# A two-layer transformer trunk on one core: the first sublayer's shift and scale as columns with the features in the partitions, applied to x r transposed beforehand

## The chip, the core and the metric

The kernel runs on one core of a Trainium2 chip. Its five engines have queues of their own and wait for each other through semaphores: TensorE (PE in the profile, its weight loads PEld), VectorE (DVE), ScalarE (ACT), GpSimd (POOL) and SyncE (SP), which here issues all DMAs. The metric is the time of one execution in microseconds (us). Everything is float32. A product of two large matrices is made of three passes with operands split into a rounded high part and the rest, the low part (type fp32r, "hi" and "lo" below); a matmul of plain float32 operands takes two passes on PE.

## What is computed

A trunk of two layers, 256 tokens of 1024 features, each layer of three sublayers: a SwiGLU, a mixer, a SwiGLU. Each sublayer normalises x, modulates it with a shift and a scale that come from one conditioning vector c, and adds its gated output to x. What the change touches is the modulation of the very first sublayer:

```
mod = silu(c) @ ada_w[i] + ada_b[i]                      # (1, 9 * 1024)
sh0, sc0, g0, sh1, sc1, g1, sh2, sc2, g2 = jnp.split(mod, 9, axis=-1)
h = rmsnorm(x, pre_norm[i, 0]) * (1.0 + sc0) + sh0       # rmsnorm(x, g) = x * rsqrt(mean(x*x) + eps) * g
y = swiglu(h, ffn_w_gate[i, 0], ffn_w_up[i, 0], ffn_w_down[i, 0])
x = x + 0.5 * g0 * rmsnorm(y, post_norm[i, 0])
```

## The kernel before

The 256 tokens are two tiles of 128 (t = 0, 1), X[0] and X[1], with the tokens in the partitions. A product needs its input transposed: HT holds h with the features in the partitions, for each tile, hi and lo, and eight blocks k of 128 features. `mm` (L267) multiplies HT's block k with a weight tile `whl`: three passes for each half of 480 columns. A weight block of 256 rows arrives by one DMA as `raw`; ACT casts each 128 rows to hi (L234) and DVE subtracts for lo (L235), into `whl`. There are 5 `raw` and 7 `whl` buffers.

The first sublayer is special. Its shift and scale are needed before any product can start, and they are sums over 1024 rows of 2048 columns of `ada_w` (8.4 MB). They are worked out in four pieces of 256 features (`first_part`, `PIECES`), so that products of the blocks k = 2q, 2q+1 can start after piece q. A piece is loaded as four tiles `fraw` by eight DMAs of 256 KB with rows of 1 KB. Eight rows j of each partition are weighted with silu(c) (`scond`): DVE accumulates 5 or 6 of them in `facc` (L375, L379), PE the other 2 or 3 (`PEJ`) directly, with `scond` as the stationary operand spread over 128 columns (L377), so that the sum over the partitions comes out the same in all 128 partitions. Another float32 matmul adds the bias (L369), one with `ones` sums `facc` (L380). Shift and scale then lie along the free axis, 256 columns, equal in all partitions: DVE forms g = (1 + scale) pre_norm (L381, pre_norm broadcast into 128 partitions as `pnb`), ACT copies the shift (L382). For each tile t, `modulated` makes h = x g r + shift on DVE (L414, L415; r is the root from `normed`: squares on ACT, L404, L406, and a power on POOL, L407), PE transposes it block by block (L418), and `split` writes hi (ACT, L393) and lo (DVE, L394) into HT.

The products of the sublayer's first part, in the order of the code: for each k, `gate` (960 columns) and `upA` (480 columns), for the two tiles one after the other; then `upB` (the other 480 columns of up) for all k. Each is 18 passes of 480 columns for a k of gate and upA together, 144 in all, and 48 for upB.

Tiles come from pools; the order of the instructions on each engine is set by a list scheduler when the kernel is built, from the order of the code, priorities and its own estimates. Each engine then runs its list strictly in order. Background work for the later sublayers (`ada_items`: on POOL the memsets of `pg`, `g`, `sh`, L302; DMAs of `araw`; DVE, L311) is spread over the kernel by `background`.

## Time and profile before

| what | before |
|---|---|
| three runs, us | 1059.56, 1059.62, 1062.03 (median 1059.62) |
| the profiled execution, us | 1058.01 |
| its span from first to last instruction, us | 1056.2 |
| PE busy | 1015.5 us, 96% of the span |
| DVE, ACT, POOL busy | 75%, 50%, 4% |
| DMA | 249 MB, 68% of 16 engines' span |
| first product of the sublayer on PE | 19.77 us |
| last product of gate and upA | 69.6 us |

The page lists engines by busy time, then groups of instructions by line, and the chain of work that ended last. The timeline gives single instructions; a stretch of time gives each engine's busy time in it. A matmul's time in the profile overlaps that of the next one, so the pace of a row of passes is read from the distance of their starts, not from the mean of one.

### The profile page before, as it was taken

What the parts mean: (1) busy time and instruction counts of PE and PEld (TensorE: products, weight loads), DVE (VectorE), ACT (ScalarE), POOL (GpSimd) and SP (SyncE); (2) the same over time, 40 slices, a digit from 0 to 9 for tenths busy, and PEclk for the clock granted to TensorE, in tenths of its full rate; (3) what the DMA queues carried; (4) which work ended last, traced back from release to release, by engine and by line L of the source; (5) the groups of instructions that cost most, each with busy time, mean ns of one, the idle gap of its engine ahead of it and who ended that gap; (6) DMA issues with size and microseconds to landing.
All of it is one profiled execution on the core that took longest, in us unless ns stands there. A gap on an engine that the chain in (4) does not pass through costs nothing.

```text
span 1056.2 us, 15311 instructions
## 1 busy us (share of the span) xinstructions
PE 1015.5 (96%) x5936; PEld 873.6 (83%) x5936; DVE 788.6 (75%) x1121; ACT 523.8 (50%) x834; POOL 45.0 (4%) x49
## 2 busy tenths in 40 slices
PE   5999999989999999999999999999999899999997
PEld 2689997769778789998878999887777678999875
DVE  5769887989976977877688967767988575765643
ACT  3354534455575654543455544346477555544432
POOL 1000000001000200000030000001000120000000
PEclk9999999999999999999999999999999999999999
DMA  9959899986443477988757979956653443778431
GB/s 315 343 147 322 313 321 378 347 293 218 148 142 128 155 273 247 352 286 291 271 193 260 314 257 316 316 208 236 260 200 118 153 134 115 243 235 261 183 117 40
DMA packets 93732, 249.48 MB, mean 236 GB/s; under 512 B 6084, under 2 KB 24652, under 8 KB 93660
## 3 DMA queue, kind: packets, MB, share of 16 engines
q1 hardware_dynamic: 93660, 248.52, 68.1%
q8 instruction: 46, 0.75, 0.3%
q14 instruction: 26, 0.21, 0.1%
HBM read 247.44 MB, written 1.05 MB: 235 GB/s over the span
## 4 chain that ended last, share of the span: by engine, by line
PE 57%; issue 20%; DVE 4%; ACT 3%; POOL 2%; DMA 1%; POOLq 0%; DVEq 0%; ACTq 0%
PE ydown L267 15%; PE up L282 9%; PE gate L282 8%; PE gate L267 3%; PE up L267 3%; PE projQd L267 2%; PE projQ L267 2%; PE projV L267 2%; PE projA L267 2%; PE projK L267 2%; PE ydsa L267 1%; POOL rstd L407 1%; DVE whl L235 1%; PE dsaO L752 1%; PE ydiff L267 1%
## 5 line engine op out<-in xcount | busy, mean ns | idle before, releaser
L235 DVE TENSOR_TENSOR whl<-raw,whl 128x1024 fp32r<-128x1024 f32 (+3 forms) x216 | 245.7, 1150 | 98.5 <-ACT whl L234 97.7
L234 ACT CAST whl<-raw 128x1024 fp32r<-128x1024 f32 (+3 forms) x216 | 211.8, 995 | 190.1 <-PE ydown L267 89.5
L282 PE MATMUL gate<-HT,wj 128*128 128x256 f32 x1344 | 166.2, 284 | 1.5 <-DVE wj L212 1.4
L212 DVE TENSOR_TENSOR wj<-raw,wj 128x1024 fp32r<-128x1024 f32 x112 | 134.7, 1221 | 43.1 <-ACT wj L211 42.8
L211 ACT CAST wj<-raw 128x1024 fp32r<-128x1024 f32 x112 | 116.4, 1050 | 100.3 <-DMA raw<-in_ffn_w_up_dram 21.5
L282 PEld LDWEIGHTS gate<-HT,wj 128*128 128x128 f32 x1344 | 163.4, 192 | 2.2 <-DVE wj L212 1.9
L282 PE MATMUL up<-HT,wj 128*128 128x256 f32 x1344 | 164.4, 283 | 0.0
L282 PEld LDWEIGHTS up<-HT,wj 128*128 128x128 f32 x1344 | 162.8, 192 | 0.4
L267 PE MATMUL ydown<-whl,ffj 128*128 128x512 f32 x672 | 157.0, 390 | 2.2 <-DVE whl L235 2.2
L267 PEld LDWEIGHTS ydown<-whl,ffj 128*128 128x128 f32 x672 | 125.7, 188 | 30.6 <-DVE whl L235 3.1
L267 PE MATMUL gate<-whl,HT 128*128 128x480 f32 x384 | 94.3, 392 | 0.4 <-ACT HT L393 0.2
L267 PE MATMUL ydown<-whl,ffa 128*128 128x512 f32 (+1 forms) x368 | 89.3, 393 | 1.9 <-ACT whl L234 1.9
L267 PEld LDWEIGHTS gate<-whl,HT 128*128 128x128 f32 x384 | 72.2, 191 | 16.6 <-ACT HT L393 2.7
L267 PEld LDWEIGHTS ydown<-whl,ffa 128*128 128x128 f32 (+1 forms) x368 | 67.9, 188 | 19.7 <-issue 3.6
L311 DVE SCALAR_TENSOR_TENSOR pg<-araw,scond,pg 128x1024 f32<-128x1024 f32 x48 | 61.4, 1280 | 6.4 <-DMA araw<-in_ada_w_dram 5.8
L267 PE MATMUL up<-whl,HT 128*128 128x480 f32 x288 | 66.0, 381 | 0.0
L267 PEld LDWEIGHTS up<-whl,HT 128*128 128x128 f32 x288 | 53.5, 188 | 8.4 <-ACT sg L512 0.5
L311 DVE SCALAR_TENSOR_TENSOR g<-araw,scond,g 128x1024 f32<-128x1024 f32 x40 | 51.2, 1281 | 7.8 <-DMA araw<-in_ada_w_dram 7.4
L311 DVE SCALAR_TENSOR_TENSOR sh<-araw,scond,sh 128x1024 f32<-128x1024 f32 x40 | 51.2, 1280 | 1.3 <-DMA araw<-in_ada_w_dram 0.8
L468 POOL TENSOR_TENSOR rstdy<-rstdy,mhalf 128x1 f32<-128x1 f32 x12 | 10.2, 850 | 824.2 <-ACT rstdy L467 824.2
L267 PE MATMUL projV<-whl,HT 128*128 128x512 f32 x96 | 28.4, 416 | 0.0
L267 PE MATMUL projQ<-whl,HT 128*128 128x512 f32 x96 | 27.6, 415 | 0.0
(224 smaller groups left out, 1090.7 us busy)
## 6 DMA issues: line engine op xcount, KB each, us to landing
araw<-in_ada_w_dram SPq DMA_DIRECT2D x64, 1024.0 KB
raw<-in_ffn_w_down_dram SPq DMA_DIRECT2D x40, 1024.0 KB
raw<-in_ffn_w_gate_dram SPq DMA_DIRECT2D x56, 512.0 KB
raw<-in_ffn_w_up_dram SPq DMA_DIRECT2D x56, 512.0 KB
raw<-in_ffn_w_gate_dram SPq DMA_DIRECT2D x16, 960.0 KB
raw<-in_diff_w_in_dram SPq DMA_DIRECT2D x12, 1024.0 KB
raw<-in_ffn_w_up_dram SPq DMA_DIRECT2D x12, 960.0 KB
fraw<-in_ada_w_dram SPq DMA_DIRECT2D x32, 256.0 KB
```

The costliest lines, as they stand in the source:

```text
L211: nc.scalar.copy(hl[0], raw)
L212: nc.vector.tensor_tensor(hl[1], raw, hl[0].bitcast(F32), op=OP.subtract)
L234: nc.scalar.copy(hl[:, 0, 0:n], raw[:, j, 0:n])
L235: nc.vector.tensor_tensor(hl[0:r, 1, 0:n], raw[0:r, j, 0:n], hl[0:r, 0, 0:n].bitcast(F32), op=OP.subtract)
L267: nc.tensor.matmul(acc[:, hf, 0:n], lhs, rhs, start=(first and hf not in seen), stop=(last and i % 3 == 2))
L282: nc.tensor.matmul(a[:, b, :], w[:, wp, j, b * 128:(b + 1) * 128], HT[:, :, hp, k0 + j, :], start=(first and j == 0 and i == 0 and b % 2 = ...
L311: nc.vector.scalar_tensor_tensor(a, raw[:, j, :], scond[:, 2 * i + j:2 * i + j + 1], a, op0=OP.mult, op1=OP.add)
L407: nc.gpsimd.tensor_tensor(r, r, mhalf[:, 0:1], op=OP.pow)
L468: nc.gpsimd.tensor_tensor(r, r, mhalf[:, 0:1], op=OP.pow)
L752: nc.tensor.matmul(flat(O)[:, h * 64:(h + 1) * 64], ptb[u][:, i * nb + b, :], v[:, b, :], start=(b == 0), stop=(b == nb - 1), skip_group_c ...
```

## The change

Shift and scale are no longer worked out as rows that are equal in all partitions, but as columns: one number for each feature, with the feature in the partition. `column_sums` makes `fraw` or `facc` the stationary operand, block by block of 128 features, and the single column `scond[:, j]` or `ones` the moving one, so each gives one column of shift or scale (a 128x1 matmul). `PEROWS` says which rows j go to PE: one of eight in the first two pieces, two of eight in the others. There are five pieces now: 128, 128, 256, 256, 256 features; the DMAs of the first two carry 128 KB with rows of 512 bytes.

The bias and pre_norm come as 24 rows of 128 (`frows`) and are turned into columns by one transpose (`fcol`). x is loaded first, multiplied by r (`xr`) and transposed by PE, 16 blocks, before the first piece (`first_x`); ACT copies the blocks to `xT`. A block of h is then one DVE operation on `xT` with scale and shift as per-partition scalars, for both tiles together (128x256); ACT writes hi and DVE lo from it. The transposes between the pieces (L418), the row operations L381, L382, L414, L415, the broadcast load of pre_norm and the tiles `g`, `sh`, `pn` of this sublayer are gone.

```
-PEJ = [3, 2, 2, 3]
-PIECES = [(i * 256, 256) for i in range(4)]
+PIECES = [(0, 128), (128, 128), (256, 256), (512, 256), (768, 256)]
+PEROWS = [(7,), (7,), (3, 7), (3, 7), (3, 7)]
...
         a = tmp("facc", (128, 2, n))
-        ps = flat(tr_tile("ps_mod0"))[:, 0:2 * n]
-        r = f0 // 256
-        nc.tensor.matmul(ps, ident[0:4, r:r + 1].to_broadcast([4, 128]),
-                         m["rows"][:, :, f0 % 256:f0 % 256 + n], start=True, stop=False)
+        ps = flat(tr_tile("ps_mod0"))[:, 0:2 * m]
+        begun = False
+
+        def column_sums(block, by, stop=False):
+
+            nonlocal begun
+            for part in range(2):
+                for k in range(m):
+                    o = part * m + k
+                    nc.tensor.matmul(ps[:, o:o + 1], block[:, part, k * 128:(k + 1) * 128], by, start=not begun,
+                                     stop=stop, skip_group_check=True)
+                    begun = True
+
+        first = True
         for j in range(8):
             rj = raws[j // 2][:, j % 2]
             sj = scond[:, j:j + 1]
-            if j == 0:
+            if j in PEROWS[q]:
+                column_sums(rj, sj)
+            elif first:
                 nc.vector.tensor_scalar(a, rj, sj, None, op0=OP.mult)
-            elif j >= 8 - PEJ[q]:
-                nc.tensor.matmul(ps, sj.to_broadcast([128, 128]), flat(rj), start=False, stop=False)
+                first = False
             else:
                 nc.vector.scalar_tensor_tensor(a, rj, sj, a, op0=OP.mult, op1=OP.add)
-        nc.tensor.matmul(ps, ones, flat(a), start=False, stop=True)
-        nc.vector.scalar_tensor_tensor(m["g"][:, c], ps[:, n:2 * n], 1.0, pn, op0=OP.add, op1=OP.mult)
-        nc.scalar.copy(m["sh"][:, c], ps[:, 0:n])
+        column_sums(a, ones[:, 0:1], stop=True)
+        k0 = f0 // 128
+        mc = small.tile([128, 2, m], F32, name="modc")
+        nc.vector.tensor_tensor(mc, ps.rearrange("p (a k) -> p a k", a=2), fcol[:, 0:2, k0:k0 + m], op=OP.add)
+        nc.vector.tensor_tensor(mc[:, 1], mc[:, 1], fcol[:, 2, k0:k0 + m], op=OP.mult)
+        h = tmp("h", (128, m, 2, 128))
+        for k in range(m):
+            nc.vector.tensor_scalar(h[:, k], FIRST["xT"][(k0 + k) // 4][:, (k0 + k) % 4], mc[:, 1, k:k + 1],
+                                    mc[:, 0, k:k + 1], op0=OP.mult, op1=OP.add)
+            hi, lo = HT[:, :, 0, k0 + k, :], HT[:, :, 1, k0 + k, :]
+            nc.scalar.copy(hi, h[:, k])
+            nc.vector.tensor_tensor(lo, h[:, k], hi.bitcast(F32), op=OP.subtract)
...
+    def first_x():
...
+        for u in range(2):
+            r, _ = normed(u)
+            xr = tmp("xr")
+            nc.vector.tensor_scalar(xr, X[u][:, 0:D], r, None, op0=OP.mult)
+            for q in range(2):
+                ps = tr_tile("ps_x")
+                for j in range(4):
+                    nc.tensor.transpose(ps[:, j, :], xr[:, (4 * q + j) * 128:(4 * q + j + 1) * 128], ident)
+                nc.scalar.copy(xT[q][:, :, u, :], ps)
```

Where the scheduler puts the work, at three places (line numbers of after are those of the changed file).

DVE at the start of the kernel, before: from the constants to the first weight tile (`facc` is the first piece's sum).

```order
L375 TENSOR_SCALAR facc<-fraw,scond 128x512
L379 SCALAR_TENSOR_TENSOR facc<-fraw,scond,facc 128x512 x3
L100 TENSOR_SCALAR ident<-jp 128x128
L103 TENSOR_SCALAR negc<-jp 128x128
L379 SCALAR_TENSOR_TENSOR facc<-fraw,scond,facc 128x512
L381 SCALAR_TENSOR_TENSOR g<-ps_mod_125,pnb_110 128x256
L414 TENSOR_TENSOR h<-x_79,g 128x256
L414 TENSOR_TENSOR h<-x_81,g 128x256
L415 SCALAR_TENSOR_TENSOR h<-h,rstd,sh 128x256 x2
L235 TENSOR_TENSOR whl<-raw,whl 128x960
```

DVE at the same place after: `xr` is x r, `whl` are the first four weight tiles of gate and up and then two of the next gate block, `modc` the first piece's columns.

```order
L450 TENSOR_SCALAR xr<-x_79,rstd 128x1024
L445 COPY fcol<-ps_f 128x24
L446 TENSOR_SCALAR fcol<-fcol 128x8
L450 TENSOR_SCALAR xr<-x_81,rstd 128x1024
L235 TENSOR_TENSOR whl<-raw,whl 128x960 x2
L235 TENSOR_TENSOR whl<-raw,whl 128x480 x2
L378 TENSOR_SCALAR facc<-fraw,scond 128x256
L235 TENSOR_TENSOR whl<-raw,whl 128x960
L381 SCALAR_TENSOR_TENSOR facc<-fraw,scond,facc 128x256
L235 TENSOR_TENSOR whl<-raw,whl 128x960
L381 SCALAR_TENSOR_TENSOR facc<-fraw,scond,facc 128x256 x5
L385 TENSOR_TENSOR modc<-ps_mod_175,fcol 128x2
```

The first piece's sum stood ahead of all weight tiles and now stands behind four of them, with two more in its midst.

POOL at the start, before (`rstd` is r of a tile; `pg`, `g`, `sh` the background's memsets).

```order
L98 IOTA jp 128x128
L407 TENSOR_TENSOR rstd<-rstd,mhalf 128x1 x2
L302 MEMSET pg 128x1024
L302 MEMSET g 128x1024
L302 MEMSET sh 128x1024
```

POOL after.

```order
L98 IOTA jp 128x128
L418 TENSOR_TENSOR rstd<-rstd,mhalf 128x1
L302 MEMSET pg 128x1024
L302 MEMSET g 128x1024
L302 MEMSET sh 128x1024
L418 TENSOR_TENSOR rstd<-rstd,mhalf 128x1
```

The second tile's r now stands behind three memsets.

ACT from the first blocks of HT on, before (`sh` is the shift of pieces 2 to 4; casts of 960 columns are gate's weight tiles, of 480 columns up's).

```order
L234 CAST whl<-raw 128x960
L382 COPY sh<-ps_mod_219 128x256
L234 CAST whl<-raw 128x960
L234 CAST whl<-raw 128x480 x2
L393 CAST HT<-ps_x 128x256 x2
L234 CAST whl<-raw 128x960
L382 COPY sh<-ps_mod_313 128x256
L234 CAST whl<-raw 128x960
L234 CAST whl<-raw 128x480 x2
L393 CAST HT<-ps_x 128x256 x2
L234 CAST whl<-raw 128x960 x2
L382 COPY sh<-ps_mod_407 128x256
```

ACT after, from the casts of the second gate block on (HT rows: pieces 1 and 2, then 3 and 4, then 5).

```order
L234 CAST whl<-raw 128x960 x2
L392 CAST HT<-h 128x2x128 x2
L234 CAST whl<-raw 128x480 x2
L392 CAST HT<-h 128x2x128 x4
L234 CAST whl<-raw 128x960 x2
L234 CAST whl<-raw 128x480 x2
L392 CAST HT<-h 128x2x128 x2
L234 CAST whl<-raw 128x960 x2
L234 CAST whl<-raw 128x480 x5
```

The casts of the third and the fourth gate block (960 columns) stood ahead of the HT blocks of the piece before their use and now stand behind them.

## Rows read from the trace of the kernel before

**Rows 1.** The first part of the page: busy time of each engine over the whole span, its share, and its instructions.
```profile
PE 1015.5 (96%) x5936; PEld 873.6 (83%) x5936; DVE 788.6 (75%) x1121; ACT 523.8 (50%) x834; POOL 45.0 (4%) x49
```

**Rows 2.** Busy time of each engine in stretches of 20 us (PE, PEld, DVE, ACT, POOL; then the granted clock of TensorE, the busy share of the DMA engines and GB/s).
```profile
100.00:120.00 20.00, 20.00 (x166) 19.83 (x165) 18.13 (x24) 8.01 (x10) 0.00 (x0) 1.00 0.81 283
...
140.00:160.00 20.00, 18.57 (x150) 18.12 (x149) 18.45 (x19) 8.68 (x10) 0.00 (x0) 1.00 0.99 356
160.00:180.00 20.00, 17.89 (x92) 14.27 (x91) 14.49 (x14) 9.33 (x11) 0.00 (x0) 1.00 1.03 369
180.00:200.00 20.00, 19.12 (x82) 14.81 (x81) 18.03 (x17) 8.28 (x9) 0.00 (x0) 1.00 0.99 382
```

**Rows 3.** The same view in a stretch of 4 us, where the DMA engines fill up again.
```profile
136.00:140.00 4.00, 4.00 (x36) 4.00 (x35) 2.79 (x3) 2.32 (x3) 0.00 (x0) 1.00 1.01 363
```

**Rows 4.** The same view in stretches of 2 us: the rates of single kinds of transfer (x with rows of 4 KB at 12 us, the slices of `ada_w` with rows of 1 KB at 28 us, a weight block with rows of 3.75 KB at 34 us) and the time after the last of the first transfers.
```profile
12.00:14.00 2.00, 2.00 (x3) 0.97 (x4) 0.00 (x0) 0.14 (x1) 0.00 (x0) 1.00 1.03 418
...
28.00:30.00 2.00, 2.00 (x7) 1.02 (x6) 0.14 (x1) 0.20 (x1) 0.00 (x0) 1.00 1.11 350
...
34.00:36.00 2.00, 2.00 (x11) 1.75 (x10) 2.00 (x6) 0.00 (x0) 0.00 (x0) 1.00 1.03 398
...
54.00:56.00 2.00, 2.00 (x9) 1.43 (x8) 1.20 (x2) 0.75 (x2) 0.00 (x0) 1.00 0.00 0
```

**Rows 5.** The timeline of the first 20 us (start, time, engine, line, operation, out<-in, count; in brackets the idle time before and what ended it).
```profile
1.60 3.99 SPq L361 DMA_DIRECT2D fraw<-in_ada_w_dram  x8
...
5.36 0.49 DVE L375 TENSOR_SCALAR facc<-fraw,scond 128x512 f32<-128x512 f32 x1 [3.81 <-DMA fraw<-in_ada_w_dram]
...
11.87 4.38 PE L377 MATMUL ps_mod<-fraw,scond 128*128 128x512 f32 x6
...
13.86 0.63 ACT L404 ACTIVATE junk<-x 128x512 f32<-128x512 f32 x1 [11.29 <-DMA x<-in_x_dram]
...
15.23 0.30 ACT L406 ACTIVATE rstd<-ss 128x1 f32<-128x1 f32 x1
...
15.61 0.56 POOL L407 TENSOR_TENSOR rstd<-rstd,mhalf 128x1 f32<-128x1 f32 x1 [14.54 <-ACT rstd L406]
...
17.66 0.95 POOL L302 MEMSET pg<- 128x1024 f32 x1
...
18.55 0.95 POOL L302 MEMSET g<- 128x1024 f32 x1
...
19.77 2.02 PE L267 MATMUL gate<-whl,HT 128*128 128x480 f32 x8
```

**Rows 6.** The timeline from 50 to 70 us: the last piece of the modulation, its transposes and what follows on PE.
```profile
51.06 2.84 PE L377 MATMUL ps_mod<-fraw,scond 128*128 128x512 f32 x6
...
63.55 1.27 PEld L267 LDWEIGHTS gate<-whl,HT 128*128 128x128 f32 x6
...
64.85 0.62 PEld L267 LDWEIGHTS upB<-whl,HT 128*128 128x128 f32 x3
...
68.97 0.82 PE L267 MATMUL upA<-whl,HT 128*128 128x480 f32 x3
```

**Rows 7.** One stretch, 19.77 to 69.60 us, five times, each row of the instructions that touch one tile alone: `gate`, `upA`, `upB`, `ps_mod`, `ps_x` in this order (length; PE busy with the count of matmul passes; PEld; the others).
```profile
19.77:69.60 49.83, 26.79 (x96) 17.64 (x96) 2.07 (x4) 1.00 0.81 273
...
19.77:69.60 49.83, 13.63 (x48) 9.01 (x48) 0.66 (x1) 1.00 0.81 273
...
19.77:69.60 49.83, 3.34 (x12) 2.36 (x13) 0.00 (x0) 1.00 0.81 273
...
19.77:69.60 49.83, 12.66 (x26) 4.49 (x26) 1.27 (x3) 1.12 (x3) 1.00 0.81 273
...
19.77:69.60 49.83, 2.19 (x12) 1.33 (x12) 3.00 (x8) 2.52 (x7) 1.00 0.81 273
```

**Rows 8.** A short stretch with the instructions of tile `dsaO` alone (length; PE, PEld, DVE busy with counts), and below it the group of this tile's weight loads by form (count, busy us, mean ns).
```profile
296.52:296.91 0.39, 0.39 (x4) 0.39 (x4) 0.00 (x0) 1.00 0.00 0
...
L752 PEld LDWEIGHTS dsaO<-vdsa,PP 128*128 128x128 f32 x96 | 12.4, 191 | 1.8 <-ACT PP L746 0.8
```

**Rows 9.** Groups by form on DVE (line, operation, shapes, count, busy us, mean ns, idle time before). L853 is an operation with two per-partition scalars on one column.
```profile
L235 DVE TENSOR_TENSOR whl<-raw,whl 128x960 fp32r<-128x960 f32 x56 | 64.2, 1154 | 18.3 <-ACT whl L234 18.2
...
L235 DVE TENSOR_TENSOR whl<-raw,whl 128x480 fp32r<-128x480 f32 x16 | 9.9, 653 | 2.7 <-ACT whl L234 2.6
...
L853 DVE TENSOR_SCALAR rsd<-rsd,sums,lamneg 128x1 f32<-128x1 f32 x16 | 4.3, 272 | 0.3
...
L415 DVE SCALAR_TENSOR_TENSOR h<-h,rstd,sh 128x256 f32<-128x256 f32 x8 | 3.5, 478 | 0.0
...
L394 DVE TENSOR_TENSOR HT<-ps_x,HT 128x256 fp32r<-128x256 f32 x8 | 3.0, 417 | 0.0
```

**Rows 10.** Groups by form on ACT (the same columns).
```profile
L234 ACT CAST whl<-raw 128x960 fp32r<-128x960 f32 x56 | 55.3, 996 | 35.5 <-PE gate L267 19.3 <-DMA raw<-in_ffn_w_gate_dram 10.7 <-PE up L267 3.3
...
L234 ACT CAST whl<-raw 128x480 fp32r<-128x480 f32 x16 | 9.1, 595 | 3.2 <-PE gate L267 1.4 <-DVE whl L235 0.8 <-ACT whl L234 0.7
...
L393 ACT CAST HT<-ps_x 128x256 fp32r<-128x256 f32 x8 | 2.9, 374 | 2.5 <-PE ps_x L418 2.4
```

**Rows 11.** The timeline around 236 us, where PE comes back after an idle time, and under it the busy time of the engines from 236 to 240 us (columns as in the stretches above; PEclk is the last number but two).
```profile
236.22 1.77 PE L418 MATMUL ps_x<-ident,h 128*128 128x128 f32 x8 [3.39 <-DVE h L415]
...
236.00:240.00 4.00, 3.78 (x16) 3.54 (x17) 3.73 (x7) 2.64 (x5) 1.47 (x2) 0.61 0.55 218
```

More of the change, by code (lines that the diff above doesn't have):

```diff
@@ L347, in first_part @@
         f0, n = PIECES[q]
+        m = n // 128
         c = slice(f0, f0 + n)
-        m = MOD[0]
-        if q == 0:
-            m["rows"] = big("abrow", (4, 2, 256))
-            nc.sync.dma_start(m["rows"], ada_b[0:1, 0:2048].rearrange("o (a q n) -> (o q) a n", a=2, n=256))
-            mod_tile(0, "g")
-            mod_tile(0, "sh")
-            m["pn"] = big("pnb0", (128, 1024))
         raws = []
@@ L362, in first_part @@
             raws.append(raw)
-        if f0 % 512 == 0:
-            nc.sync.dma_start(m["pn"][:, f0:f0 + 512], bcast_rows(pre_norm[0, 0, f0:f0 + 512], 512))
-        pn = m["pn"][:, c]
         a = tmp("facc", (128, 2, n))
-        ps = flat(tr_tile("ps_mod0"))[:, 0:2 * n]
-        r = f0 // 256
-        nc.tensor.matmul(ps, ident[0:4, r:r + 1].to_broadcast([4, 128]),
-                         m["rows"][:, :, f0 % 256:f0 % 256 + n], start=True, stop=False)
+        ps = flat(tr_tile("ps_mod0"))[:, 0:2 * m]
[9 more added lines that the diff above has]
+        first = True
         for j in range(8):
@@ L421, in trunk @@
     FIRST = {}
+    fcol = consts.tile([128, 3, 8], F32, name="fcol")
+    def first_x():
+        for u in range(2):
+            nc.sync.dma_start(X[u][:, 0:D], x[0, u * 128:(u + 1) * 128, :])
+        rows = big("frows", (24, 128))
+        nc.sync.dma_start(rows[0:16, :], ada_b[0:1, 0:2048].rearrange("o (r n) -> (o r) n", n=128))
+        nc.sync.dma_start(rows[16:24, :], pre_norm[0, 0:1, :].rearrange("o (r n) -> (o r) n", n=128))
+        FIRST["xT"] = xT = [big("xT", (128, 4, 2, 128)) for _ in range(2)]
+        ps = flat(tr_tile("ps_f"))
+        nc.tensor.transpose(ps[:, 0:24], rows, ident[0:24, 0:24])
+        nc.vector.tensor_copy(fcol.rearrange("p a k -> p (a k)"), ps[:, 0:24])
+        nc.vector.tensor_scalar(fcol[:, 1], fcol[:, 1], 1.0, None, op0=OP.add)
+        for u in range(2):
+            r, _ = normed(u)
[6 more added lines that the diff above has]
+                nc.scalar.copy(xT[q][:, :, u, :], ps)
     def first_h(t, k):
+        if not FIRST:
+            first_x()
         for q, (f0, n) in enumerate(PIECES):
@@ L428, in first_h @@
                 first_part(q)
-                if q == 0:
-                    FIRST["x"] = []
-                    for u in range(2):
-                        nc.sync.dma_start(X[u][:, 0:D], x[0, u * 128:(u + 1) * 128, :])
-                        FIRST["x"].append(normed(u))
-                for u in range(2):
-                    modulated(0, u, *FIRST["x"][u], k, n // 128)
-        return FIRST["x"][t][1]
+        return HT[:, t]
     def prenorm(t, n):
```

## The prediction

> **What bounds the kernel now.** I read the page first: PE is busy 96% of the span [rows 1], so nothing is gained off PE unless PE waits for it. Then the stretches: from 100 to 120 us PE has no gap; from 140 to 200 us the DMA engines are full and PE stands idle 4.4 of 60 us [rows 2]. That full stretch begins at 136 us [rows 3], after SP has waited for buffers that DVE and PE free, so a PE that is late there makes it begin late. A change ahead of 70 us should therefore reach the end nearly one for one.
>
> The change lies ahead of 70 us. Before the first product at 19.77 us PE waits for the first piece of shift and scale [rows 5]. From there to the end of gate and upA (68.97 us and three passes, so 69.6) [rows 6] I count PE's work: 96 + 48 + 12 passes of 480 columns, 26 float32 passes of 512 columns for the modulation, 12 transposes [rows 7]. Six 480-column passes start 1.30 us apart from the next row's [rows 6], 0.216 each: 33.7 us. Six modulation passes take 2.84, the last one drawn 0.59 long [rows 6], so 0.44 each: 11.4 us. The transposes take about 0.11 each (their loads 1.33 for 12) [rows 7]: 1.3 us. Sum 46.4 of 49.8 us: PE is idle only 3.4 us, and this stage is bound by PE. DMA is not what ends it: the first transfers are over by 52 us, and nothing moves at 54 us [rows 4].
>
> **The change, part by part.**
>
> *Modulation on PE.* Removed behind the first product: 26 passes and 12 transposes, 12.7 us. Added: 44 one-column products (4 each for the two pieces of 128, 12 each for the three of 256), of which 4 precede the first product; 40 remain, each of two passes. No 128x1 product stands in the trace. The nearest row is `dsaO`, 64 columns: four passes in 0.39 us, although a load of its weights is drawn 0.19 long [rows 8]; so 0.195 for a product and 7.8 us in all. Bounds: 0.1 a pass, and 0.19 if each load ran alone. Fewer columns cannot need more than 64 do, hence the low end. PE's work becomes 33.7 + 7.8 = 41.5 us, 4.9 less.
>
> The Trainium skill (TensorE: Matmul & The Clock Gate, The mechanism) says that a weight load overlaps with running matmuls only when it goes to another row group; here all use all rows. By that rule the 80 passes would cost 15.2 us. The four in 0.39 us speak against it in this kernel.
>
> *The first product.* x comes first now. The first 0.5 MB before were asked for from 1.60 us and used at 5.36 [rows 5]; x has longer rows and a higher rate (418 against 350 GB/s) [rows 4], so I take 4.5 us for its first tile. Squares and sum take 1.67 us on ACT (13.86 to 15.53), the power 0.56 on POOL [rows 5]: r of tile 0 at 6.8. The second r now stands behind three POOL memsets, 0.89 apart [rows 5]: 9.5, and ready at 10.1; x r of 1024 columns is two operations like L375, 0.97 [rows 9]: DVE is free at 11.0. Its list then holds, ahead of the first piece's end, four gate tiles (1.15 each), two up tiles (0.65), one start of the sum (0.3) and six accumulations of 256 columns (0.44, half a pair like L415) [rows 9]: 4.6 + 1.3 + 0.3 + 2.6 = 8.8, plus 0.6 for casts of up that stand behind ACT's copies to `xT`: 20.4. Then the four passes of the last products at the slow clock (below) 0.8, two small operations 0.3, h with two scalars 0.4 (0.27 for one column, and half of L375 as the other bound) [rows 9], the cast 0.4 [rows 10]: **first product at 22.4 us, 2.6 later than before.** Data are there sooner: rows of 1 KB and 3.75 KB move at 350 and 398 GB/s [rows 4], which gives 47 and 154 ns a row on one of 16 engines and, on that line, 27 for 512 bytes, 300 GB/s. With x, 2.5 MB of weights and 2.1 MB of the first two pieces these end at 15.3 and 18.8 us. Bounds for the first product: 19.8 (as before) to 24.
>
> *The clock.* In the first 15 us six passes take 4.38 us where later 2.84 do [rows 5, 6], and at 236 us, after 3.39 us without work, eight transposes take 1.77 us and the granted clock of 4 us is 0.61 [rows 11]: 1.2 instead of 2.4 GHz for about 3 us. Before, this time lay ahead of the first product, in work that waited for DMA. Now PE has only 17 transposes up to about 13 us and stands idle until 20.4, so I expect the lower level under the first products, for 3 to 5 us, of which half is lost: 2.0 (0 to 2.6).
>
> *New waits of PE.* A piece's columns wait for PE's own last products, and h waits for them. Ahead of k = 2: small operations 0.3, one weight tile of up that DVE's list puts between (0.65), h 0.4, cast 0.4 [rows 9, 10]: 1.8 us with nothing else ready. Ahead of k = 4: 11 passes of k = 3 (2.4 us) cover the same chain, but the third gate block is now cast behind it (1.0) and its low half comes 1.15 later [rows 9, 10]; what sticks out is 0.8. Ahead of k = 6: only two passes (0.4) are left to cover 0.3 + 0.4 + two casts of HT 0.8 + one of gate 1.0, so 2.1, and 0.7 more for the low half: 2.8. Sum 5.4 (2 to 8); what the trace of before has is 3.4 in the same stretch.
>
> *What costs nothing.* The copies to `xT` and 17 transposes lie where PE and ACT waited before. The three additional accumulations on DVE replace longer row operations. Without the broadcast of pre_norm (0.5 MB, 1.4 us at 370 GB/s) DMA ends earlier, and nothing waits for it; were DMA the bound, this would be the gain.
>
> **Sum.** 22.4 + 41.5 + 2.0 + 5.4 = 71.3 against 69.6: 1.7 us later. The profiled execution takes 1058.0, so 1059.7; the median of the runs is 1.6 higher, so 1061.3.
>
> **Rivals.**
>
> *Faster.* The weights are cast in time after all and the clock stays up, because DMA lands earlier than the chain needs. Waits 3.4 as before and no loss of clock give −4.0: 1057.3. With the first product at 19.8 as well, 1054.7. For it speaks that 4.9 us of PE's work do go; against it the lists: ACT's casts of gate stand behind HT's, and a list is strict.
>
> *Slower: one-column products cost a full load.* At 0.19 a pass 80 passes take 7.4 us more: 1068.7. It decides from about 0.12 a pass on. The rows of `dsaO` speak against it. This is also what the skill's rule above would give.
>
> *Slower: the first pieces land late.* 16 DMAs of 128 KB stand in SP's list where 8 of 256 KB stood. If their number, not their bytes, set the pace, they run at 175 GB/s and the second piece lands at 11.8 + 12 = 23.8 us; PE's list has a product with its last rows ahead of the first product of gate: 24.0, so 1.6 more, 1062.9.
> The Trainium skill (DMA: Bandwidth & Descriptors, Measured) gives 138 GB/s for 64 KB and 341 for 1 MB; as an estimate between these, 128 KB would also run near half speed. The 350 GB/s at 256 KB speak against it, since transfers here run in parallel.
>
> *Nothing arrives.* The full DMA stretch from 136 us starts when it did, and 4.4 us of idle PE in it [rows 2] swallow the difference: 1059.6.
>
> **How the numbers follow.** The measurement tells 0.3%, 3.2 us, from no change. Chances: the sum above 0.5, with 1058 to 1064.5 as its own range by the bounds of the clock, the waits and the first product; faster 0.25; costly products 0.1; late pieces 0.1; nothing arrives 0.05. Below 1056.4 lie most of the faster case and little of the first: 0.22. Above 1062.8 lie the costly products, half of the late pieces or more, and the first case's upper end: 0.3. The rest is 0.48. Range 1055.5 to 1066: it cuts off the end of the faster case and the costly products.
>
> **What would show it.** Right: in the profile after, the first product of gate at 22 to 23 us, its passes at about 0.4 for some 4 us; rows of four one-column passes starting about 0.1 apart; PE idle ahead of k = 2 and k = 6 by ACT's or DVE's weight tiles; the last pass of upA near 71 us, and the same difference at 240 us. Wrong: a first product before 21 us, no slow passes, or gate's tiles ready ahead of HT, which would make it faster; one-column passes of 0.15 or more, which would make it slower.

## The result and the profile after

The changed kernel takes 1064.35 us, the median of 20 runs (1059.41 to 1069.36), against 1057.74 of the kernel before, also in 20 runs: a ratio of 1.0065 with an interval of 1.0053 to 1.0077. It is 6.6 us slower; the sum had said 1.7. The profiled execution takes 1063.4 us (span 1061.6), 5.4 more than that of before. Three runs well above the others of their kernel are left out of all figures over several runs below: 3474.58 us of the kernel before, 2536.2 of e4 and 1094.8 of e3.

The first line of the page:

```profile
PE 1010.5 (95%) x5989; PEld 877.2 (83%) x5989; DVE 795.1 (75%) x1133; ACT 524.7 (49%) x835; POOL 44.7 (4%) x49
```

PE is busy 5.0 us less than in [rows 1], in a span that is 5.4 us longer: the change did take work off PE, and PE stands still or runs slowly for longer.

The timeline ahead of the first product, which answers to [rows 5]:

```profile
5.06 0.63 ACT L415 ACTIVATE junk<-x 128x512 f32<-128x512 f32 x1 [2.38 <-DMA x<-in_x_dram]
...
7.30 0.95 POOL L302 MEMSET pg<- 128x1024 f32 x1
7.39 3.19 DVE L450 TENSOR_SCALAR xr<-x,rstd 128x1024 f32<-128x1024 f32 x1 [5.53 <-POOL rstd L418]
...
9.08 0.95 POOL L302 MEMSET sh<- 128x1024 f32 x1
10.00 0.99 POOL L418 TENSOR_TENSOR rstd<-rstd,mhalf 128x1 f32<-128x1 f32 x1
...
10.94 0.95 POOL L302 MEMSET pg<- 128x1024 f32 x1
11.02 2.30 DVE L450 TENSOR_SCALAR xr<-x,rstd 128x1024 f32<-128x1024 f32 x1
...
13.30 1.16 DVE L235 TENSOR_TENSOR whl<-raw,whl 128x960 fp32r<-128x960 f32 x1
...
20.49 2.56 DVE L381 SCALAR_TENSOR_TENSOR facc<-fraw,scond,facc 128x256 f32<-128x256 f32 x5
...
23.11 1.01 PE L367 MATMUL ps_mod<-ones,facc 128*128 128x1 f32 x4 [6.24 <-DVE facc L381]
...
24.99 0.40 ACT L392 CAST HT<-h 128x256 fp32r<-128x256 f32 x1 [6.20 <-DVE h L389]
...
25.44 2.77 PE L267 MATMUL gate<-whl,HT 128*128 128x480 f32 x6 [0.90 <-ACT HT L392]
...
28.01 1.24 PE L267 MATMUL upA<-whl,HT 128*128 128x480 f32 x3
```

The first product of gate starts at 25.44 us. DVE has x r in its queue from 7.39 to 13.3 us, because each of the two operations runs beside GpSimd's memsets of background work: the first ends 0.55 us after the third memset (10.58 against 10.03). The first six passes start 2.57 us apart from the next row's, 0.43 each: the lower clock.

PE around the waits ahead of k = 2 and k = 6, which answers to [rows 6], and the work of ACT and DVE in the second wait:

```profile
37.41 1.07 PEld L367 LDWEIGHTS ps_mod<-ones,facc 128*128 128x128 f32 x8
37.62 0.95 PE L367 MATMUL ps_mod<-ones,facc 128*128 128x1 f32 x8
...
40.36 1.57 PE L267 MATMUL gate<-whl,HT 128*128 128x480 f32 x6 [1.79 <-ACT HT L392]
...
60.87 0.95 PE L367 MATMUL ps_mod<-ones,facc 128*128 128x1 f32 x8
61.68 0.68 PE L267 MATMUL upA<-whl,HT 128*128 128x480 f32 x2
64.37 3.57 PE L267 MATMUL gate<-whl,HT 128*128 128x480 f32 x8 [2.01 <-ACT whl L234]
```

```profile
62.69 0.73 ACT L392 CAST HT<-h 128x256 fp32r<-128x256 f32 x2 [9.65 <-DVE h L389]
...
63.33 4.35 ACT L234 CAST whl<-raw 128x960 fp32r<-128x960 f32 x7
```

Eight one-column passes start 0.81 us before the next row (60.87 to 61.68), 0.10 each. Both waits are there. And the eight gate passes at 64.37 take 3.57 us, 0.42 from start to start, where 0.216 is the pace at the full clock. In stretches (columns as in [rows 2]):

```profile
60.00:64.00 4.00, 2.36 (x16) 1.86 (x15) 1.81 (x6) 1.31 (x3) 0.00 (x0) 0.88 0.02 4
64.00:68.00 4.00, 3.63 (x9) 3.08 (x10) 3.65 (x5) 3.68 (x7) 0.00 (x0) 0.50 0.13 13
68.00:72.00 4.00, 4.00 (x16) 3.21 (x15) 1.83 (x4) 1.03 (x2) 0.00 (x0) 0.76 0.91 308
```

The granted clock is 0.50 here: 1.2 GHz, from 63.1 to 69.9 us by the trace's record of it. Before, no stretch between 15 us and 236 us was at the lower level. That record begins when the clock first rises, at 28.9 us here and at 15.0 before. What lies ahead of it is listed as 1.00, although the passes from 25.44 us on are slow:

```profile
25.40:28.90 3.50, 3.46 (x9) 2.90 (x10) 3.01 (x7) 0.00 (x0) 0.00 (x0) 1.00 0.91 292
```

The rates of DMA behind x (answering to [rows 4]):

```profile
12.00:18.00 6.00, 3.53 (x15) 2.70 (x13) 5.07 (x7) 5.73 (x10) 0.78 (x1) 1.00 1.21 295
...
26.00:50.00 24.00, 22.21 (x122) 19.64 (x121) 15.55 (x35) 2.58 (x7) 0.00 (x0) 1.00 1.02 349
```

The rows of 512 bytes moved at 295 GB/s; the estimate was 300. By the packets in the trace those of the first piece end at 15.4 us and those of the second at 19.8; the forecast was 15.3 and 18.8.

The last pass of upA starts at 77.3 us, so the stage ends at 77.5; before it was 69.6. That is 7.9 us later. At `projA` (248.1 against 237.6 us) the difference is 10.5, at `ydsa` (308.0, 297.6) 10.4, at `projK` (741.0, 733.4) 7.6, at `ydiff` (836.9, 828.5) 8.4. In part the changes on the way are further stretches at half clock: this execution has them at 165.5 and 182.5 us, where that of before has none (the difference grows by 2.7 us there), and before has them at 349.5 and 830.8 us, where this one has none (it falls by 0.9 and 1.6).

The difference also falls slowly, by 4.1 us in all, in the gate and up products of later sublayers (394 to 490, 588 to 690 and 903 to 990 us of before), where PE is busy throughout and the granted clock is 1.00 in both. The first of these stretches, before and then after, with the same passes but two:

```profile
394.00:490.00 96.00, 96.00 (x746) 93.35 (x744) 74.65 (x75) 43.90 (x49) 0.00 (x0) 1.00 0.86 301
```

```profile
403.80:498.60 94.80, 94.80 (x744) 92.18 (x744) 74.70 (x75) 43.86 (x49) 0.00 (x0) 1.00 0.87 305
```

In the last of them the passes of 256 columns start 0.117 us apart in the median, before 0.120. There is one trace of the kernel before, so whether this belongs to the kernel or to the execution stays open.

### The profile page after: what moved, and what is told of

It reads as the page before. It is cut to its first block, busy times and chain, and to the rows that moved or that the text cites. A ratio compares the mean times of both kernels' runs of the same rounds, so it can differ in the third digit from the quotient of the medians.

```text
span 1061.6 us, 15435 instructions
## 1 busy us (share of the span) xinstructions
PE 1010.5 (95%) x5989; PEld 877.2 (83%) x5989; DVE 795.1 (75%) x1133; ACT 524.7 (49%) x835; POOL 44.7 (4%) x49
## 3 DMA queue, kind: packets, MB, share of 16 engines
q1 hardware_dynamic: 95584, 248.00, 68.2%
## 4 chain that ended last, share of the span: by engine, by line
PE 63%; issue 20%; DVE 6%; DMA 5%; ACT 4%; POOL 2%; DVEq 0%; POOLq 0%; SPq 0%; ACTq 0%
PE ydown L267 15%; PE gate L282 8%; PE up L282 8%; PE gate L267 6%; PE up L267 4%; DMA araw<-in_ada_w_dram 3%; PE projQd L267 2%; PE projQ L267 2%; PE projV L267 2%; PE projA L267 2%; PE projK L267 2%; PE ydsa L267 1%; DMA fraw<-in_ada_w_dram 1%; POOL rstd L418 1%; DVE whl L235 1%
## 5 line engine op out<-in xcount | busy, mean ns | idle before, releaser
L282 PE MATMUL up<-HT,wj 128*128 128x256 f32 x1344 | 162.1, 281 | 0.8 <-ACT wj L211 0.8
L282 PEld LDWEIGHTS up<-HT,wj 128*128 128x128 f32 x1344 | 160.6, 189 | 1.4 <-ACT wj L211 1.0
L267 PEld LDWEIGHTS gate<-whl,HT 128*128 128x128 f32 x384 | 72.6, 194 | 19.8 <-ACT HT L392 3.1
```

The costliest lines, as they stand in the source:

```text
L267: nc.tensor.matmul(acc[:, hf, 0:n], lhs, rhs, start=(first and hf not in seen), stop=(last and i % 3 == 2))
L282: nc.tensor.matmul(a[:, b, :], w[:, wp, j, b * 128:(b + 1) * 128], HT[:, :, hp, k0 + j, :], start=(first and j == 0 and i == 0 and b % 2 = ...
```

## The clock over all runs

Each run lists its mean granted clock. Over the 20 runs of the changed kernel it is 0.9906 in the mean, over 55 runs of the kernel before (those beside e1 to e11 below) 0.9949. These means hold the record alone, that is the time behind the first rise: the 0.991 listed for the profiled execution is what the stretches of its record at half clock make. One minus the clock, times the time, gives 10.0 and 5.4 us. Within either kernel the runs lie along a line, with correlations of 0.89 and 0.94: each us of that quantity goes with 0.73 us (after) and 0.93 us (before) of time. So 4.6 us more of it are worth 3.4 to 4.3 us, an estimate from these slopes: half to two thirds of the 6.6 us. The rest, 2.3 to 3.2 us, stands between runs of the two kernels at the same listed clock: at 0.996 two runs after take 1059.69 us in the mean and 13 before 1055.89; at 0.992 two take 1063.06 and three 1060.75. In this rest lie, by the one trace, the 1.7 us at half clock under the first products, from 25.4 to 28.9 us, which no mean holds; before, the clock rose ahead of the first product.

## Experiments

Theory after the result: x r beside the memsets makes the first product late, and stretches at half clock behind the waits for a piece cost what the sum had only once. Rivals: the one-column products cost more than they look; the waits alone; the landing of rows. The kernel before ran beside each group, so ratios are compared; "first" is the start of the first gate product, "end" that of the last pass of upA, "half clock" the stretches at the lower level between 28 and 80 us, all three in the one profiled execution; "clock" is the mean over the runs. In the traces of e6, e10 and e11 the clock is up at 12 us and falls again from 15 us to 22.4 or 25.4, so their record holds time that in the others lies ahead of it: their means are too low to be set beside the rest.

| kernel | median, us | ratio to before | first | end | half clock, us | clock |
|---|---|---|---|---|---|---|
| before | 1057.74 | | 19.8 | 69.4 | none | 0.9949 |
| after | 1064.35 | 1.0065 (1.0053 to 1.0077) | 25.4 | 77.3 | 63.1–69.9 | 0.9906 |
| e1 | 1064.73 | 1.0066 (1.0043 to 1.0089) | 23.8 | 78.4 | 40.2–43.6, 64.1–71.0 | 0.9911 |
| e2 | 1063.25 | 1.0047 (1.0029 to 1.0065) | 25.3 | 75.0 | 42.2–45.6 | 0.9917 |
| e3 | 1078.29 | 1.0217 (1.0181 to 1.0252) | 26.2 | 98.1 | 35.3–55.8, 62.6–69.4 | 0.9818 |
| e4 | 1063.28 | 1.0056 (1.0036 to 1.0076) | 26.1 | 76.9 | 40.9–44.3, 64.8–68.2 | 0.9912 |
| e5 | 1063.40 | 1.0059 (1.0038 to 1.0079) | 25.2 | 77.6 | 39.2–46.0 | 0.9926 |
| e6 | 1060.44 | 1.0024 (1.0000 to 1.0049) | 22.3 | 77.1 | 39.0–42.5, 62.9–69.8 | 0.9905 |
| e7 | 1064.22 | 1.0086 (1.0056 to 1.0116) | 25.3 | 78.4 | 40.2–43.7, 67.6–71.0 | 0.9915 |
| e8 | 1062.37 | 1.0073 (1.0047 to 1.0100) | 22.6 | 75.6 | 64.3–67.8 | 0.9874 |
| e9 | 1065.46 | 1.0077 (1.0049 to 1.0104) | 21.4 | 82.6 | 31.0–34.5, 41.3–44.7, 54.9–58.4, 68.6–75.4 | 0.9890 |
| e10 | 1061.07 | 1.0037 (1.0016 to 1.0057) | 17.9 | 73.7 | 36.0–42.9, 46.3–49.7 | 0.9866 |
| e11 | 1063.51 | 1.0053 (1.0021 to 1.0086) | 18.0 | 73.9 | 36.1–46.3 | 0.9856 |
| e12 | 1058.16 | 1.0006 (0.9989 to 1.0024) | 25.3 | 71.3 | none | 0.9947 |

**e1, memsets behind both r.**

```
-            nc.gpsimd.memset(a, 0.0)
+            with tc.issue_after(FIRST["r1"]):          # the second power on GpSimd
+                nc.gpsimd.memset(a, 0.0)
...
```

> The changed kernel with one edge more: the three background memsets on POOL are queued behind both powers of r. If these memsets slow the multiplication x r on DVE (3.19 and 2.30 us in the changed kernel, against 0.98 expected) and hold up the second r, x r takes about 1 us each and the first product of gate comes near 22.5 instead of 25.44 us; the time falls by 2 to 3 us, to about 1061.5. If x r is dear by itself, it stays above 2 us, only the wait for the second r goes, and the time falls by about 1 us.

Its timeline, x r without and with memsets beside it:

```profile
7.18 0.75 DVE L453 TENSOR_SCALAR xr<-x,rstd 128x1024 f32<-128x1024 f32 x1 [5.31 <-POOL rstd L419]
...
8.64 0.95 POOL L303 MEMSET pg<- 128x1024 f32 x1
8.72 2.30 DVE L453 TENSOR_SCALAR xr<-x,rstd 128x1024 f32<-128x1024 f32 x1 [0.50 <-POOL rstd L419]
...
27.82 2.33 PE L267 MATMUL gate<-whl,HT 128*128 128x480 f32 x5
```

The same operation takes 0.75 us alone and 2.30 beside memsets: the cause of that delay is shown. The first product came 1.7 us sooner, at 23.77, but nothing of it arrived. In this execution the clock rose no sooner for it, at 30.0 us (the five passes at 27.82 still take 2.14 to the next row), so the first products ran slowly for 6.2 us instead of 3.5, and there is a further stretch at half clock from 40.2 us. Over its seven runs the listed clock is that of the changed kernel, so that stretch is not the whole reason; the rest is not shown.

**e2, a piece's weight casts ahead of its blocks of HT** (for k = 2, 4 and 6).

```
+        if q > 1:
+            b0 = 2 * (q - 1)
+            for b in (b0, b0 + 1):
+                W[b] = make_block(b)
...
+                with tc.issue_after(CAST[2 * (q - 1)]):
+                    nc.scalar.copy(hi, h[:, k])
```

> The changed kernel with the casts of the second up block and of the third and fourth weight blocks queued on ACT ahead of the blocks of HT of their piece, nothing else. If the place of these casts makes PE wait (0.45, 0.46 and 2.01 us) and the wait ahead of k = 6 is what drops the clock from 63 to 70 us, these waits and the slow passes after them go: 5 to 6 us less, about 1058.5. If PE is held by its own products or the weights are late for another reason, less than 1 us changes.

PE around k = 2 and k = 6:

```profile
38.17 0.58 PE L372 MATMUL ps_mod<-scond,fraw 128*128 128x1 f32 x4
40.66 1.58 PE L268 MATMUL gate<-whl,HT 128*128 128x480 f32 x6 [1.91 <-ACT HT L399]
...
65.20 0.49 PE L268 MATMUL upA<-whl,HT 128*128 128x480 f32 x1 [0.72 <-DVE whl L236]
...
66.10 0.70 PE L268 MATMUL gate<-whl,HT 128*128 128x480 f32 x2 [0.20 <-DVE HT L402]
```

The wait ahead of k = 6 fell from 2.01 to 0.92, and the clock stayed up there; it fell behind the wait ahead of k = 2 instead, which the edit had not shortened. The end of upA came 2.3 us sooner, the time 1 to 2, with intervals that overlap; 5 to 6 had been expected.

**e3, every one-column product twice** (the sums come out doubled).

```
+                    for _ in range(2):
                         nc.tensor.matmul(ps[:, o:o + 1], block[:, part, k * 128:(k + 1) * 128], by, ...
```

> The changed kernel with each one-column product issued twice into the same sum (so shift and scale are computed from doubled sums; not what the reference has). 88 further passes, at the 0.124 us that they are apart in the changed kernel: 10.9 us if every one counts; four of the 44 products lie where PE waits anyway, so 9 to 10 us, about 1074. If one-column products hide in PE's waits, under 3 us. If a doubled stream also ran each pass at a full load of 0.19, 16 us.

One stretch of it:

```profile
40.00:56.00 16.00, 14.21 (x52) 12.84 (x52) 5.25 (x12) 0.73 (x2) 0.00 (x0) 0.51 0.63 210
```

It cost 16 us by the ratios and 14 by the medians, not 9 to 10; by the time alone a full load of 0.19 a pass would fit. The trace speaks against that (its own length, 1094.8 us, says little): where passes stand at the full clock they take what they took before (median distance of starts 0.112 us, as in the changed kernel), and the clock is down for most of 35 to 56 us. As an estimate, 88 more passes at 0.097 are 8.5 us, and 9.7 us more of lost clock at the slope of 0.73 are 7.1: 15.6. That many of these products go with a lower clock is what the rows show.

**e4, PE kept busy ahead of the first product** (36 products of 480 columns whose results nobody reads, as the first weight tiles arrive).

```
+            if b < 3:
+                for i in range(WARM[b][j]):
+                    nc.tensor.matmul(warmp[:, 0:480], onesr, hl[:, 0, 0:480], start=True, stop=True, ...
```

> The changed kernel with 36 products of 480 columns more, of ones with the first weight tiles, into a PSUM tile that nobody reads; they stand on PE between the transposes of x r and the first product. If the first products run slowly because PE stood idle before, their passes are 0.216 instead of 0.4 us apart and the time falls by 1.7 to 2 us, to about 1062.5. If the slow passes have another cause (weights arriving, the first sums), they stay, and the time stays or rises with the work added.

The clock is up from 17.0 us, so the first products ran at full pace, but they start 0.7 us later, and two stretches at half clock follow. The loss at the first products is real, about 1.7 us; bought back alone it gives about 1 us, with intervals that overlap.

**e5, wide work in the wait ahead of k = 6** (16 products of 256 columns that nobody reads; the order of all else is that of the changed kernel).

```
+        if q == 4:
+            extra = flat(tr_tile("extra"))
+            for i in range(16):
+                with tc.issue_after(FIRST["end"].ins):
+                    FIRST["fill"] = nc.tensor.matmul(extra[:, 0:256], onesr, HT[:, :, 0, 0, :], ...
```

> Adds 16 products of 256 columns, whose results nobody reads, behind the last one-column products of the last piece, in the place where TensorE waits 2.0 us for k = 6; the order of everything else is that of the changed kernel. Theory: the granted clock falls at 63 us because TensorE stands still there behind one-column products. With wide work in the wait it stays at the full level from 29 to 100 us, the last pass of upA ends 2.5 to 3 us sooner, near 75 us, and the time is 2 to 3 us below the changed kernel's (1064). The 16 products cost at most 1.8 us at the full clock, against a wait of 2.0. Rival: the one-column products lower the clock whatever follows them; the half level still stands at 63 to 70 us, and the time is 1064 to 1066.

PE, and two stretches:

```profile
37.48 0.94 PE L367 MATMUL ps_mod<-ones,facc 128*128 128x1 f32 x8
40.21 2.77 PE L267 MATMUL gate<-whl,HT 128*128 128x480 f32 x6 [1.79 <-ACT HT L398]
...
64.15 2.02 PE L387 MATMUL extra<-HT,onesr 128*128 128x256 f32 x15
```

```profile
42.00:46.00 4.00, 4.00 (x12) 3.31 (x11) 3.47 (x5) 0.00 (x0) 0.00 (x0) 0.50 1.08 379
...
66.00:70.00 4.00, 3.84 (x18) 2.71 (x17) 3.54 (x6) 4.00 (x7) 0.00 (x0) 1.00 0.00 0
```

With the wait filled the clock stays at 1.00 behind it. But up to 60 us this list is that of the changed kernel, and here the clock fell at the wait ahead of k = 2 (39.2 us), where in the changed kernel's execution, after the same wait of 1.79 us, it did not. So neither side had it whole: whether a given wait costs a stretch at half clock differs from one execution to the next, and one trace doesn't tell a kernel's loss. The time fell by 0.6 to 1 us, not by 2 to 3. From here on I read the clock over all runs.

**e6, the first piece on PE alone, memsets behind both x r.**

```
-PEROWS = [(7,), (7,), (3, 7), (3, 7), (3, 7)]
+PEROWS = [tuple(range(8)), (7,), (3, 7), (3, 7), (3, 7)]
...
+            if u:
+                seen = small.tile([128, 1], F32, name="seen")
+                FIRST["xr"] = nc.gpsimd.tensor_copy(seen, xr[:, 0:1]).ins      # memsets issue after it
```

> The first piece's shift and scale are summed by TensorE alone (16 one-column products as its rows land; no accumulation on VectorE), and GpSimd's background memsets wait until both x r are made. Theory: the first product came at 25.4 us because VectorE was late (x r beside memsets 3.2 and 2.3 us, then the accumulations). Then it starts at 20 to 22 us here, each x r takes 0.75, and the end of upA comes 4 us sooner, near 73.5; the time is about 1060. Rival: what ends the wait is the landing of the rows, at 21 us or later, and the time gained is taken back by another stretch at half clock, as with the memsets moved alone: 1062 to 1065.

PE ahead of the first product:

```profile
14.38 6.57 PE L368 MATMUL ps_mod<-scond,fraw 128*128 128x1 f32 x32 [2.09 <-ACT whl L234]
...
22.28 2.77 PE L267 MATMUL gate<-whl,HT 128*128 128x480 f32 x6 [1.33 <-ACT HT L394]
```

Both x r take 0.75 us, and the first product starts at 22.3: the 3 us are gone. The profiled execution gave them back, to a wait ahead of k = 1 (0.79 us for ACT's HT at 29.55 us, because DVE's list has the second piece's sums only behind the first piece's h, at 21.7 us), and to a further stretch at half clock; over ten runs 4 us arrived, the theory's time, though not its end of upA.

**e7, pieces a step of k early.**

```
-            if f0 == k * 128 and q not in FIRST:
+            if f0 == (k + 1 if q > 1 else k) * 128 and q not in FIRST:
```

> The pieces for k = 2, 4 and 6 are issued one step of k earlier, so that more passes stand between a piece's last one-column products and the gate pass that needs them. Theory: the waits ahead of k = 2, 4 and 6 (1.8, 0.9 and 2.0 us) fall to under 0.5 each, and with them the spell at half clock from 63 us (2.5 to 3): upA's last pass at 72 to 73 us, the time 1058 to 1060. Rival: what these passes wait for is not the pieces but the casts of gate's weights, or the rows land too late for it; then the waits stay and the time is 1063 to 1065.

The rival had it: ahead of k = 2 still 1.79 us and ahead of k = 6 still 2.01 us on ACT's cast of gate's weights (the gate row at 66.07 us), and no gain. The list kept two passes between the last sums and the gate pass that needs them.

**e8, e6 and e7 together.**

> The first piece on TensorE alone, the memsets behind both x r, and the pieces a step early, together. Theory: the gains add: 77.5 less 4 less 5 gives upA's last pass near 68 to 69 us, before the kernel before's 69.6, and a time of 1055 to 1057. Rival: the gains meet the same limit (casts of the weights on ScalarE and VectorE, or a further spell at half clock): 1058 to 1062.

The gains did not add: 1062.37, with a wait of 2.01 ahead of k = 6, about what the rival had.

**e9, the first rows ahead of the weights on SP.**

```
+        with (tc.issue_after(LAST[0 if b < 2 else 1]) if b < 4 else contextlib.nullcontext()):
             nc.sync.dma_start(raw[:, 0:full, 0:n], ...
...
         while later and p >= later[0][0]:
-            later.pop(0)[1]()
+            with tc.issue_after(LAST[4]):
+                later.pop(0)[1]()
```

(`later` is the set-up of later sublayers; it is queued behind the last piece's rows as well.)

> Only the order of SP's queue changes: the first piece's 16 rows of shift and scale stand ahead of the first weights of gate and up, the second piece's ahead of the second gate block. Theory: in the changed kernel the first product (25.4 us) waits for a chain of rows that land behind 2.5 MB of weights, then sums, then h. With the rows first the sums follow x r (VectorE is free of it at 13.3) and the first product starts at 17 to 20 us; upA's last pass comes 3 to 6 us sooner (72 to 74), the time 1058 to 1061. Rival: as with the first piece on TensorE (first product 3 us sooner, end of upA only 0.2 sooner), the gain is given back in a wait ahead of k = 1 and a further spell at half clock: upA's end at 76 to 77, 1062 to 1064.

The first product came 4 us sooner and the end of upA 5 us later; the clock was down in four stretches. Its five runs have a median of 1065.46, above the rival's 1064: the rival was right in kind and too mild.

**e10, e2, e6 and e9 together; e11, with e7 as well.**

> All that the runs so far point to: first rows ahead of the weights on SP, the first piece summed on TensorE alone, memsets behind both x r, and a piece's weight casts ahead of its blocks of HT on ScalarE and VectorE. Theory: everything ahead of k = 2 comes earlier, with a first product at 14 to 17 us; TensorE's work is about 41 us behind it, with 5 us of waits and half clock that gives upA's last pass at 61 to 66 us against 69.6 in the kernel before, and a time of 1050 to 1055. Rival: from k = 2 on the landing of rows and weights sets the pace (the transfers end near 50 us in every kernel so far), so that TensorE waits longer at k = 2, 4 and 6, the clock falls in the waits, and upA's last pass comes at 68 to 72: 1057 to 1060.

> The kernel of the run before with the pieces for k = 2, 4 and 6 issued one step of k earlier as well. Theory: if the waits ahead of k = 4 and 6 are for a piece's chain (sums, h, cast), they shrink and the time is 1 to 2 us below that run. Rival: they are for casts and landings, and the two kernels agree within 1 us.

In e10:

```profile
17.88 3.16 PE L271 MATMUL gate<-whl,HT 128*128 128x480 f32 x6 [2.29 <-ACT whl L238]
...
33.58 3.36 DVE L239 TENSOR_TENSOR whl<-raw,whl 128x960 fp32r<-128x960 f32 x4
33.83 0.70 PE L271 MATMUL gate<-whl,HT 128*128 128x480 f32 x2 [1.33 <-ACT HT L404]
...
36.85 0.76 DVE L407 TENSOR_TENSOR HT<-h,HT 128x256 fp32r<-128x256 f32 x2
37.33 1.17 PE L271 MATMUL gate<-whl,HT 128*128 128x480 f32 x2 [1.83 <-DVE HT L407]
37.38 2.38 ACT L238 CAST whl<-raw 128x960 fp32r<-128x960 f32 x3 [3.28 <-DMA raw<-in_ffn_w_gate_dram]
```

The first product is at 17.9 us, ahead of the kernel before, and the end of upA still 4.3 us behind it. At k = 2 PE waits 1.33 us for a piece's h and its cast, and 1.83 for the low halves, which DVE's list now has behind four weight tiles (33.58 to 36.85): the edit moved the wait. ACT does wait for a landing (37.38), but no row shows PE waiting behind it, so that the landings set the pace, as the rival had it, is not shown. In this execution PE is at half clock under the first products to 22.4 us and again from 36.0 to 42.9 and 46.3 to 49.7. The time, 1061.07, is above both forecasts. e11 is no faster than e10 (1063.51, intervals that overlap).

**e12, each product 64 columns wide, of which one is used.**

```
-                    nc.tensor.matmul(ps[:, o:o + 1], block[...], by, start=not begun,
+                    nc.tensor.matmul(ps[:, o * 64:(o + 1) * 64], block[...],
+                                     by.to_broadcast([128, 64]), start=not begun,
```

> Each one-column product takes its moving column 64 times (64 columns, of which one is used), with the same weights and the same sums. A 64-column float32 product takes 0.39 us where a one-column product takes about 0.195, so the 40 behind the first gate product add up to 8 us of work. Theory: the granted clock falls because TensorE has stretches in which it loads weights for a single column and then waits; with 64 columns the mean granted clock over all runs goes from 0.9906 (changed kernel, 20 runs) to about 0.995 (kernel before), and the time is 1064.5 plus 8 less 3 to 4, so 1068 to 1069. Rival: the waits alone lower it, whatever the products ahead of them; the mean clock stays at 0.990 to 0.991 and the time is 1071 to 1073.

PE around k = 6, and the stretches that answer to those of the changed kernel:

```profile
57.01 1.00 PE L367 MATMUL ps_mod<-ones,facc 128*128 128x64 f32 x8
57.82 0.47 PE L267 MATMUL upA<-whl,HT 128*128 128x480 f32 x1
58.13 1.46 PE L267 MATMUL gate<-whl,HT 128*128 128x480 f32 x6
59.42 0.81 PE L267 MATMUL upA<-whl,HT 128*128 128x480 f32 x3
60.57 2.33 PE L267 MATMUL gate<-whl,HT 128*128 128x480 f32 x8 [0.33 <-ACT whl L234]
```

```profile
60.00:64.00 4.00, 3.62 (x16) 2.65 (x15) 3.55 (x6) 3.88 (x7) 0.00 (x0) 1.00 0.06 8
64.00:68.00 4.00, 4.00 (x19) 3.29 (x19) 2.49 (x5) 1.63 (x3) 0.00 (x0) 1.00 0.92 298
```

Both expectations were wrong on the cost, it seems by a misread row: the 0.39 us of [rows 8] are four passes, two products, as the prediction had it. Eight passes of 64 columns start 0.81 us before the next row, exactly as eight of one column. The clock is right as the theory had it: no stretch at half clock from 28 to 240 us, and a mean of 0.9947 over 12 runs, that of the kernel before. And the time is 1058.16, 6 us below the changed kernel and the same as before.

It is not the width alone, though. The scheduler rates the wider products differently and wrote another list: ten passes now stand between the last sums and the gate of k = 6, where two stood, and the waits are 0.33 us there and 0.67 ahead of k = 2, instead of 2.01 and 1.79. By the slope of the changed kernel's runs, 0.9947 instead of 0.9906 is worth 4.4 x 0.73 = 3.2 us; the other 3 of the 6 would be the shorter waits themselves. Whether the width or the waits keep the clock up is not separated; a kernel with this list and one column was not tried. One trace bears on it: in e2 single columns, with 13 passes of 480 columns between the last sums of the last piece and a wait of 0.92 us, left the clock up at k = 6.

## Why the prediction came out as it did

The time lies in the range, and on the slower side, for reasons that the sum had in kind but not in size. That it lies inside is in part luck: the range was built on 1059.62 us, the median of three runs before, and over 20 runs, those three among them, it is 1057.74. As a difference the range ended at 6.4 us, and 6.6 were measured. The steps of the sum, up to the end of upA (71.3 forecast, 77.5 measured):

| term | forecast | measured |
|---|---|---|
| first product | 22.4 | 25.4 |
| 156 passes of 480 columns | 33.7 | 33.9 (0.217 each at the full clock) |
| 40 one-column products | 7.8 | 7.6 (39 products, since one of the second piece stands ahead of the first product; 77 distances of their 78 passes, all but the one with a wait, add up to 7.49: 0.097 each) |
| waits | 5.4 | 4.7 (1.79 + 0.91 + 2.01; those of 0.91 by the weight loads) |
| clock | 2.0 | 4.5 (1.7 up to 28.9 us, 2.8 from 63.1 to 69.9) |
| rest | 0 | 1.4 in small gaps |

- *PE's work* is right, and with it the value taken from `dsaO` [rows 8]. The rival of a full load of 0.19 for each pass is refuted by 0.10 a pass; the drawn 0.19 is not a price, since eight loads at 37.41 us take 1.07 together. By the rule of the Trainium skill weighed there (TensorE: Matmul & The Clock Gate, The mechanism) no load would be covered, since all use all rows; the trace disagrees with it, as from 26 to 50 us PE is busy 22.21 and its loads 19.64 of 24.00 us.
- *The waits* are where the prediction put them, at k = 2, 4 and 6, and for the reasons given: ACT's cast of HT, and of gate's weights behind it. With them and with the clock down, the rival *faster* is out.
- *The first product* is the first term that failed. The step that failed is "x r of 1024 columns is two operations like L375, 0.97". The memsets were counted as standing ahead of the second power on POOL, not as slowing DVE beside them; alone x r takes 0.75 (e1, e6), beside them 3.19 and 2.30. With DVE free at 13.3 us instead of 11.0 the same sum gives a first product at 24.7. (Two slips of the working change little: its last steps add up to 22.3, and the 0.49 of L375 stands in [rows 5].) The Trainium skill (SBUF — State Buffer, Who interferes with whom) says that VectorE in a two-port mode and GpSimd exclude each other for a whole instruction; the trace agrees in that the first x r ended 0.55 us after the third memset; which mode x r runs in, no run here shows.
- *The clock* is the second. The prediction had the loss under the first products right (1.7 for 2.0) and saw no other, although it forecast the waits that came before the others. The runs put the clock behind its first rise at 3.4 to 4.3 us of the difference; the 1.7 under the first products stand beside them. The Trainium skill (TensorE: Matmul & The Clock Gate, HAM oscillation — how this bites in real kernels) tells of a kernel whose clock falls again in the waits between its groups of products; the rows at 64.37 us show the same here behind a wait of 2.01, though it is not so at every such wait (e5).
- *Late pieces*, a rival, is not what held the first product: the rows came at 295 GB/s and of both first pieces were there at 19.8 us, and the last sums of the first piece, at 23.11, waited for DVE, not for DMA. With DVE out of the way (e6) the first product starts at 22.3.
- *Nothing arrives* is refuted: 7.9 us at 77.5 us are 10.5 at 248, behind the full DMA stretch, and 5.4 to 6.6 at the end.

What stays open: whether width or waits decide on the clock (e12 moved both), why the same list loses it at one wait in one execution and at another in the next, and where the gain of e1 went over its runs.

## What to carry to other kernels

A change that replaces steady work of TensorE by less work and more waits should be charged for the clock at every new wait, not once, and over many runs: the mean granted clock of each run tells it for the time behind its first rise, one trace does not. Before an operation of VectorE is moved, look at what GpSimd does at that time. And where TensorE's operand is a single column, try a wider one: 64 columns cost nothing here, and the kernel with them was 6 us faster, though by its other order or by the width is not separated. Last, a scheduler that builds the lists from its own estimates may answer a change of shape with another order of everything around it, so read the lists again.

## What was not expected of the hardware

- A float32 product of 64 columns costs the same as one of a single column: 0.10 us a pass in both (0.81 for eight). The prediction had assumed it from [rows 8]; e12 shows it.
- A first product that comes sooner did not bring the rise of the clock sooner by as much: 25.4 and 28.9 us in the changed kernel, 23.8 and 30.0 in e1, 21.4 and 27.6 in e9, one execution each.
- x r of 128x1024 takes 0.75 us alone and 2.30 to 3.19 beside GpSimd's memsets.
- The same list of instructions, with the same wait of 1.79 us, went with 6.8 us at 1.2 GHz in one execution (e5) and with none in another (the changed kernel).
